# One layer of a hybrid encoder on one core: scaling of attention probabilities and masked decay tiles moved to VectorE, a second inverse tile, another order of DeltaNet pieces

## The chip, the cores and the metric

The kernel runs on one core of one Trainium2 chip. The time is device time in microseconds (us) of one launch. TensorE (PE in the profile) multiplies, VectorE (DVE), ScalarE (ACT) and GpSimd (POOL) do everything elementwise, SyncE (SP) issues all DMA transfers of this kernel in one queue. PEld is TensorE's loading of weights, which runs beside its matmuls.

## The reference

One layer with 1024 tokens of width 1024 in float32: a mixer (windowed attention and a bidirectional gated DeltaNet side by side, from one input projection), cross attention into 256 memory tokens, and a SwiGLU network, each with normalisation and residual. The change lies in the mixer:

```python
h = _rms_norm(x, g_mix_pre); proj = h @ w_in            # 1024 x 1024 @ 1024 x IN_COLS
# windowed attention, 8 heads, 2 key/value heads, blocks of 128, +-1 block:
scores = jnp.where(mask, einsum(q, k) * 64 ** -0.5, -inf)
m = max(max(scores), sink); p = exp(scores - m)
o = einsum(p / (sum(p) + exp(sink - m)), v)
...
# DeltaNet, 4 heads of 128, both directions, chunks:
q, k, v = silu(conv5(proj[...])), q and k L2-normalised
g = cumsum(-exp(a_log) * softplus(a + dt_bias)); beta = sigmoid(bt)
decay = exp(where(lower_triangle, g[i] - g[j], -inf))
lower = strict_lower((k * beta) @ k.T * decay); tmat = lower + I
u, w = tmat^-1 @ [v * beta, k * beta * exp(g)]
qk = q @ k.T * decay
scan over chunks: v_new = u - w @ S; o = q exp(g) @ S + qk @ v_new; S = S * g_last + kg.T @ v_new
...
mix = concat([attn_o, dn_o]) @ w_out; x += norm(mix); then cross attention, then SwiGLU
```

## The kernel before

Every large product is written as three fp32r matmuls of a high and a low part (`hhi,whi`, `hlo,whi`, `hhi,wlo`); `whi` is cast on ScalarE (L103) and `wlo` subtracted on VectorE or GpSimd (L104). The input projection is cut into pieces of 128 output columns (`proj`, matmuls at L260, 1056 of 128x128 by 128x512 after the first stage), and between these pieces stands the work that uses them.

The program is written as lists of pieces, and a tile scheduler reorders the instructions of each engine from that text, the tiles' pools and its own idea of durations. ORDER_1 holds the DeltaNet preparation; a letter with a head's number is one piece: q, k and v are projection plus convolution (`delta_proj`: copies and scaled sums, L282 to L286), E the decays, K the turned keys, U the key products (to `d_u` in memory), S the beta rows of two heads, C the query products (to `d_pz` and `d_kv`), B the inverse of the 32 x 32 diagonal blocks of two heads. ORDER_2 holds the attention projections A, V, the gate G, the levels L (which put together the full inverse of a head from B's blocks, in memory `d_inv`) and windows W, two windows at a time. ORDER_3 holds the scans with the remaining windows between them. Then come the output projection (L1029), cross attention and the SwiGLU network, which the change doesn't touch.

`decays(h)` makes, for both halves b of the chunks and both directions, a mask tile times one column per chunk, for the high and the low part of g: tile `gm` (128 x 4 x 128), eight tiles for a head. TensorE multiplies each with a triangular matrix (L471), four into one bank, and ScalarE takes the exponential (E, L474).

`base_inverse(g)` loads the diagonal blocks of two heads into V, makes A from them, runs 30 steps of small VectorE products (L539, L541), writes V and A once more (L543, L544) and stores both. V and A come from the pool `tb` with one buffer, so the second inverse takes the space of the first. `levels(h)` fetches the blocks again (`cz`, `cw`), makes m5, c5, c6 of them, and passes through `bs`, `z5`, `mov6` between PE and ACT or DVE (L589 to L616).

`window(n, g)` loads queries (`qr`), splits them (`qs`, the low part by GpSimd at L641), scores them (`psw`), takes the maximum on VectorE (L651), exponentials on ScalarE (L658), the reciprocal of the sum (`es`, L661 to L664), scales the four probability tiles of 128 x 384 or 128 x 256, and in a second part transposes them (`ptw`), splits them (`ph` on ScalarE L103, `pl` on VectorE L104) and multiplies with the values (`pow`, L677).

Of the kernel before, what the change touches and what calls it, by code (L numbers as in the profile page):

```python
# [10 lines left out]
F32 = mybir.dt.float32  # L11
# [3 lines left out]
ALU = mybir.AluOpType  # L15
# [4 lines left out]
P = 128  # L20
# [3 lines left out]
NT = S // P  # L24
# [9 lines left out]

ORDER_1 = ("k0 k1 q0 E0 K0 U0 E1 v0 K1 U1 S0 q1 C0 v1 E2 C1 k2 E3 k3 q2 K2 U2 v2 K3 U3 S1 q3 C2 v3 C3 B0 B1").split()
ORDER_2 = "L0 L1 G0 G1 A4 V A0 A1 L2 L3 W W W A2 A3 G2 G3 W".split()
ORDER_3 = ("M " + "s01 W K " * 5 + "s01 K " * 3 + "s01 V V").split()

# [36 lines left out]
def tile_hybrid_block(  # L77
# [6 lines left out]
    nc = tc.nc  # L84
# [9 lines left out]
    def f32(ap):  # L94
        return ap.bitcast(F32)

    def bc(ap, axis, shape):
        return ap.unsqueeze(axis).to_broadcast(list(shape))
# [10 lines left out]
    def pool(name, bufs, **kw):  # L109
        return tc.tile_pool(name=name, bufs=bufs, reuse_waits="tile", **kw)  # L110
# [28 lines left out]
    C0, C1 = _AT["mUi"], _AT["mU"]  # L139
# [14 lines left out]
    cm = {n: (C[:, a - C0:a - C0 + P] if a < C1 else CE[:, a - C1:a - C1 + P]) for n, a in _AT.items() if n != "ident"}  # L154
# [115 lines left out]
    pp_ = ExitStack()  # L270
    tb = pp_.enter_context(pool("tb", 1))
# [125 lines left out]

    pa1.close()
    pa0.close()

# [58 lines left out]
    def decays(h):  # L461

        for b in range(2):
            pa = small()
            n = 0
            for d, (mi, ml) in enumerate((("mUi", mL_r), ("mLi", mU_r))):
                for part in (ghi, glo):
                    gm = t2.tile([P, 4, P], F32R, tag="gm", name="gm")
                    for j in range(4):
                        nc.scalar.activation(gm[:, j, :], cm[mi], AF.Identity, scale=part[:, d, h, 4 * b + j:4 * b + j + 1])  # L470
                    nc.tensor.matmul(pa, ml, gm.rearrange("p c n -> p (c n)"), start=(n == 0), stop=(n == 3))  # L471
                    n += 1
            E = Es[h, b] = t2.tile([P, 4, P], F32, tag="E", name="E", bufs=4)
            nc.scalar.activation(E, pa.rearrange("p (c n) -> p c n", c=4), AF.Exp)  # L474
# [40 lines left out]
    def base_inverse(g):  # L515

        V = tb.tile([P, 32, 32], F32, tag="V", name="V", bufs=1)
        for q in range(4):  # L520
            r = slice(32 * q, 32 * q + 32)
            nc.sync.dma_start(V[q:64:4], d_u[g].rearrange("h c p n -> (h c) p n")[:, r, r])
        bB = tb.tile([P, 32], F32, tag="bB", name="bB", bufs=1)
        b1 = tb.tile([64, 32], F32, tag="b1", name="b1", bufs=1)
        bv = d_beta[g].rearrange("(d h c) (b s) -> d (h c b) s", d=2, h=2, b=4)
        for d in range(2):
            nc.sync.dma_start(bB[64 * d:64 * d + 64], bv[d])
        nc.sync.dma_start(b1, bv[1])
        A = tb.tile([P, 32, 32], F32, tag="A", name="A", bufs=1)
        nc.vector.scalar_tensor_tensor(A[0:64], V[0:64].rearrange("p r s -> p s r"), -1.0,  # L530
                                       bc(bB[0:64], 1, (64, 32, 32)), ALU.mult, ALU.mult)
        nc.vector.scalar_tensor_tensor(A[64:128], V[0:64], -1.0, bc(b1, 1, (64, 32, 32)), ALU.mult, ALU.mult)
        nc.gpsimd.affine_select(out=A, in_=A, compare_op=ALU.is_gt, fill=0.0, base=0,
                                pattern=[[1, 32], [-1, 32]], channel_multiplier=0)
        tmp = tb.tile([P, 256], F32, tag="tmpb", name="tmpb", bufs=1)
        for j in range(1, 31):
            n = 31 - j
            tv = tmp[:, 0:n * j].rearrange("p (r s) -> p r s", r=n)
            nc.vector.tensor_tensor(tv, A[:, j + 1:, j:j + 1].to_broadcast([P, n, j]),  # L539
                                    A[:, j:j + 1, 0:j].to_broadcast([P, n, j]), ALU.mult)  # L540
            nc.vector.tensor_tensor(A[:, j + 1:, 0:j], A[:, j + 1:, 0:j], tv, ALU.add)  # L541
        nc.gpsimd.memset(A.rearrange("p r s -> p (r s)")[:, 0:1024:33], 1.0)
        nc.vector.tensor_tensor(V.rearrange("p r s -> p s r"), A, bc(bB, 2, (P, 32, 32)), ALU.mult)  # L543
        nc.gpsimd.tensor_tensor(A, A, bc(bB, 2, (P, 32, 32)), ALU.mult)  # L544

        for i in range(2):
            for d in range(2):
                nc.sync.dma_start(d_inv[g][i][d].rearrange("h c b r s -> (h c b) r s"),
                                  (A if i == d else V)[64 * d:64 * d + 64])
# [77 lines left out]
    def window(n, g):  # L627

        tok = slice(n * P, (n + 1) * P)
        k0, k1 = max(n - 1, 0), min(n + 1, NT - 1) + 1  # L630
        nb = k1 - k0
        w = nb * P
        band = C[:, _AT["band0"] - C0 + (k0 - n + 1) * P:][:, 0:w]

        khi, klo = (t[:, k0 * P:k1 * P] for t in keys[g])
        qr = tw.tile([P, 4, P], F32, tag="qr", name="qr", bufs=1)
        for r in range(2):
            nc.sync.dma_start(qr[64 * r:64 * r + 64], d_q[256 * g:256 * g + 256, tok].rearrange("(h e) t -> e h t", h=4))
        qs = tw.tile([P, 4, P], F32R, tag="qs", name="qs")
        nc.scalar.copy(qs, qr)  # L640
        nc.gpsimd.tensor_tensor(qs[64:128], qr[64:128], f32(qs[64:128]), ALU.subtract)  # L641

        m4 = tw.tile([P, 4], F32, tag="m4", name="m4")
        ssum = tw.tile([P, 4], F32, tag="ssum", name="ssum")
        pr = []
        for hh in range(4):
            pp = pw.tile([P, 512], F32, tag="pw", name="psw")
            for i, kk in enumerate((khi, klo)):
                nc.tensor.matmul(pp[:, 0:w], qs[:, hh, :], kk, start=(i == 0), stop=(i == 1))
            sc = tw.tile([P, 384], F32, tag="sc", name="sc", bufs=8)  # L650
            nc.vector.tensor_tensor_reduce(out=sc[:, 0:w], in0=pp[:, 0:w], in1=band, scale=0.125,  # L651
                                           scalar=sink[:, 4 * g + hh:4 * g + hh + 1], op0=ALU.add, op1=ALU.max,
                                           accum_out=m4[:, hh:hh + 1])
            pr.append(sc)
        nm = tw.tile([P, 4], F32, tag="nm", name="nm")
        nc.vector.tensor_scalar(nm, m4, -1.0, None, ALU.mult)
        for hh in range(4):
            nc.scalar.activation(pr[hh][:, 0:w], pr[hh][:, 0:w], AF.Exp, bias=nm[:, hh:hh + 1],  # L658
                                 accum_out=ssum[:, hh:hh + 1])
        es = tw.tile([P, 4], F32, tag="es", name="es")  # L660
        nc.gpsimd.tensor_tensor(es, sink[:, 4 * g:4 * g + 4], m4, ALU.subtract)  # L661
        nc.scalar.activation(es, es, AF.Exp)
        nc.vector.tensor_tensor(es, es, ssum, ALU.add)
        nc.vector.reciprocal(es, es)  # L664
        for hh in range(4):
            nc.scalar.mul(pr[hh][:, 0:w], pr[hh][:, 0:w], es[:, hh:hh + 1])
        yield
        po = pw.tile([P, 4, P], F32, tag="pow", name="pow", bufs=1)
        for j in range(nb):
            pp = pw.tile([P, 512], F32, tag="pw", name="ptw")  # L670
            for hh in range(4):
                nc.tensor.transpose(pp[:, hh * P:(hh + 1) * P], pr[hh][:, j * P:(j + 1) * P], ident)
            ph = tw.tile([P, 512], F32R, tag="ph", name="ph")
            pl = tw.tile([P, 512], F32R, tag="pl", name="pl")
            split(ph, pl, pp)
            for i, pe_ in enumerate((ph, pl)):
                nc.tensor.matmul(po.rearrange("p h t -> p (h t)"), vhl[:, k0 + j, g].rearrange("p r e -> p (r e)"), pe_,  # L677
                                 start=(j == 0 and i == 0), stop=(j == nb - 1 and i == 1))
        ao = tw.tile([P, 4, P], F32, tag="ao", name="ao", bufs=1)[0:64]
        nc.scalar.copy(ao, po[64:128])  # L680
        nc.vector.tensor_tensor(ao, po[0:64], ao, ALU.add)
        nc.sync.dma_start(d_mix[g * 256:(g + 1) * 256, tok].rearrange("(h e) t -> e h t", e=64), ao)
# [38 lines left out]
    def issue(order, table):  # L721
        for o in order:
            table[o[0]](*(int(c) for c in o[1:]))

    issue(ORDER_1, {**{n: delta_proj(n) for n in "kqv"}, "E": decays, "K": turned_keys, "U": key_products, "S": beta_rows,
                    "C": query_products, "B": base_inverse})
# [337 lines left out]
    for hf in range(2):  # L1064
        for kp in range(4):
            k2 = slice(2 * kp, 2 * kp + 2)
# [73 lines left out]
    q0 = cross_q(0)  # L1140
    cross_attention(q0)
    q1 = cross_q(1)
# [68 lines left out]
    for e in range(EARLY):  # L1211
        f = 2 * e
        sg = te.tile([P, 512], F32, tag="sg", name="sg0")
        w, A = [], []
# [318 lines left out]
```

## Time and profile before

| | us |
|---|---|
| median of three runs | 1563.44 (1560.02 to 1566.67) |
| the profiled execution, own time | 1564.91 |
| its span (first to last instruction) | 1562.9 |
| TensorE busy | 1496.5 |
| VectorE busy | 1041.0 |
| ScalarE busy | 789.0 |
| GpSimd busy | 369.3 |
| mean granted TensorE clock | 0.988 of full speed |

A row of the timeline gives the start in us, the duration, engine, line, operation, out<-in, shapes and a count where equal instructions follow each other; in brackets stands how long the engine had been idle and what released it. Rows of waits give the total, the number and the longest. In the program of before, the lines are those of the function listing above; from the first edit on, those of the changed program are higher by 1 (from L400), 4 (from L474) and 5 to 7 (from L666).

### The profile page before, as it was taken

The page shows a single profiled execution, that of the slowest core. Times are in us where ns is not written, and L with a number is a line of the kernel's source. Part 1 is how long each engine was busy: PE and PEld are TensorE (multiplying, and loading weights), DVE is VectorE, ACT ScalarE, POOL GpSimd, SP SyncE. Part 2 cuts the span into 40 slices and gives each one's busy share as a digit, 9 for nine tenths or more (in the row PEclk, how much of TensorE's full clock was granted, in tenths as well). Part 3 has the DMA queues.
Part 4 walks back from the last instruction along what each step waited for, and adds up shares of the span by engine and source line. Part 5 has one row for each costly group of instructions (what it writes and reads, how often), then busy time and mean ns, then how long its engine had stood idle before and what let it go on. Part 6 is the DMA issues. An engine that isn't in the chain of part 4 may idle for free.

```text
span 1562.9 us, 21101 instructions
## 1 busy us (share of the span) xinstructions
PE 1496.5 (96%) x7451; PEld 1255.6 (80%) x7451; DVE 1041.0 (67%) x1664; ACT 789.0 (50%) x1634; POOL 369.3 (24%) x364
## 2 busy tenths in 40 slices
PE   6999999898899989999999999999999999999997
PEld 5877878787899877788888777888888888888786
DVE  6747989775788865444355458786867654696665
ACT  5698933357757774554345575332322322454542
POOL 3001220011236300153202221433534333000021
PEclk9999999999899999999999999999999999999999
DMA  6224575763998484454213164343434333853354
GB/s 203 75 82 124 154 202 132 175 187 122 316 279 283 136 279 175 135 198 153 68 55 126 50 222 149 121 135 121 135 115 141 101 102 133 292 194 102 108 173 163
DMA packets 264710, 242.95 MB, mean 155 GB/s; under 512 B 33800, under 2 KB 203677, under 8 KB 264605
## 3 DMA queue, kind: packets, MB, share of 16 engines
q1 hardware_dynamic: 264605, 241.62, 49.1%
q8 instruction: 58, 0.95, 0.3%
q14 instruction: 47, 0.39, 0.1%
HBM read 172.07 MB, written 66.88 MB: 153 GB/s over the span
## 4 chain that ended last, share of the span: by engine, by line
PE 66%; DVE 7%; ACT 6%; DMA 6%; issue 2%; SPq 2%; POOL 1%; DVEq 0%; POOLq 0%; ACTq 0%
PE pmg L1029 9%; PE pD L1204 8%; PE pE L1204 7%; PE pA L1204 6%; PE pcq L260 6%; PE pdX L1394 6%; PE pdA L1394 4%; PE pB L1204 4%; PE psc L798 3%; PE pdD L1394 2%; PE pg L260 2%; PE pcs L1110 1%; PE pco L1136 1%; PE pdX L1487 1%; PE pck L929 1%
## 5 line engine op out<-in xcount | busy, mean ns | idle before, releaser
L103 ACT CAST whi<-wraw 128x1024 fp32r<-128x1024 f32 x108 | 113.1, 1048 | 142.8 <-PE pmg L1029 33.7
L104 DVE TENSOR_TENSOR wlo<-wraw,whi 128x1024 fp32r<-128x1024 f32 x70 | 85.7, 1225 | 95.2 <-ACT whi L103 91.1
L260 PE MATMUL pg<-hhi,whi 128*128 128x512 f32 x352 | 140.4, 399 | 0.0
L260 PE MATMUL pg<-hhi,wlo 128*128 128x512 f32 x352 | 139.4, 396 | 0.0
L260 PE MATMUL pg<-hlo,whi 128*128 128x512 f32 x352 | 139.4, 396 | 0.0
L104 POOL TENSOR_TENSOR wlo<-wraw,whi 128x1024 fp32r<-128x1024 f32 x38 | 92.5, 2434 | 167.7 <-ACT whi L103 157.9
L1029 PE MATMUL pmg<-whi,b 128*128 128x512 f32 x384 | 118.5, 395 | 2.6 <-ACT whi L103 2.2
L1204 PE MATMUL pA<-s,whi 128*128 128x512 f32 x352 | 109.5, 392 | 1.3 <-ACT m L1221 1.3
L1029 PEld LDWEIGHTS pmg<-whi,b 128*128 128x128 f32 x384 | 71.2, 188 | 17.9 <-ACT whi L103 2.7
L260 PEld LDWEIGHTS pg<-hhi,wlo 128*128 128x128 f32 x352 | 67.0, 190 | 13.3
L260 PEld LDWEIGHTS pg<-hlo,whi 128*128 128x128 f32 x352 | 66.9, 190 | 13.2
L1394 PE MATMUL pdX<-dhl,whi 128*128 128x512 f32 x264 | 76.1, 390 | 1.5 <-ACT dhl L103 0.8
L1204 PEld LDWEIGHTS pA<-s,whi 128*128 128x128 f32 x352 | 65.3, 188 | 15.0 <-ACT m L1221 2.0
L260 PEld LDWEIGHTS pg<-hhi,whi 128*128 128x128 f32 x352 | 66.9, 190 | 13.1 <-ACT hhi L103 0.2
L103 ACT CAST whi<-araw 128x1024 fp32r<-128x1024 f32 (+1 forms) x36 | 35.4, 982 | 71.8 <-PE pdX L1394 27.6
L1029 PE MATMUL pmg<-wlo,b 128*128 128x512 f32 x192 | 71.5, 392 | 0.0
L1281 POOL TENSOR_TENSOR act<-act,up 128x512 f32<-128x512 f32 x33 | 50.2, 1520 | 88.8 <-DVE up L1280 53.5
L1204 PE MATMUL pA<-s,wlo 128*128 128x512 f32 x176 | 68.7, 391 | 1.0 <-DVE wlo L104 1.0
L104 DVE TENSOR_TENSOR wlo<-araw,whi 128x1024 fp32r<-128x1024 f32 (+1 forms) x36 | 40.8, 1134 | 39.4 <-ACT whi L103 39.3
L285 DVE SCALAR_TENSOR_TENSOR acc<-cp,cols,acc 128x1024 f32<-128x1024 f32 x48 | 63.9, 1332 | 1.4 <-ACT acc L283 0.8
L1253 POOL TENSOR_TENSOR sr<-wraw 128x512 f32<-128x512 f32 x22 | 30.4, 1381 | 127.1 <-DMA wraw<-in_w_gate_up_dram 127.1
L1394 PEld LDWEIGHTS pdX<-dhl,whi 128*128 128x128 f32 x264 | 49.3, 188 | 12.7 <-ACT dhl L103 1.1
(411 smaller groups left out, 4096.7 us busy)
## 6 DMA issues: line engine op xcount, KB each, us to landing
wraw<-in_w_gate_up_dram SPq DMA_DIRECT2D x52, 512.0 KB, 3.9
kv<-d_kv SPq DMA_DIRECT2D x32, 512.0 KB, 6.3
wraw<-in_w_in_dram SPq DMA_DIRECT2D x22, 512.0 KB, 4.1
b<-in_w_down_dram SPq DMA_DIRECT2D x20, 512.0 KB, 6.5
araw<-d_as SPq DMA_DIRECT2D x20, 512.0 KB, 3.7
pz<-d_pz SPq DMA_DIRECT2D x32, 256.0 KB, 6.7
wraw<-in_w_ckv_dram SPq DMA_DIRECT2D x16, 512.0 KB, 7.6
wraw<-in_w_out_dram SPq DMA_DIRECT2D x16, 512.0 KB, 4.1
```

Of the source, the lines that this page charges most:

```text
L103: nc.scalar.copy(hi, src)
L104: (eng or nc.vector).tensor_tensor(lo, src, f32(hi), ALU.subtract)
L260: nc.tensor.matmul(p_, w[:, k, :], ah[a][:, k, :], start=(k == 0 and i == 0), stop=(k == nk - 1 and i == 2))
L285: nc.vector.scalar_tensor_tensor(acc, cp[:, t:t + S], taps[t], acc, ALU.mult, ALU.add)
L798: nc.tensor.matmul(out[:, d, h, :], lt[:, d, h, :], rt[:, d, h, :], start=True, stop=True)
L929: nc.tensor.matmul(pp, w[:, k, :], mT[a][:, k, :], start=(k == 0 and i == 0), stop=(k == KT - 1 and i == 2))
L1029: nc.tensor.matmul(pp[t], act[a][:, k, tt], w_[:, kk, :], start=(k == 0 and i == 0), stop=(k == KT - 1 and i == 2))
L1110: nc.tensor.matmul(pp[:, t2_, :], q[a][:, ct, tt], kr_[b_][:, ct, :], start=(j == 0 and i == 0), stop=(j == 1 and i == 2))
L1204: nc.tensor.matmul(out_, w[a][:, k, :], xx[b_][:, k, :], start=(start and k == 0 and i == 0), stop=(k == HK - 1 and i == 2), skip_group_ch ...
L1253: nc.gpsimd.tensor_tensor(s[0], b_[:, 0:HK], b_[:, HK:], ALU.add)
L1281: nc.gpsimd.tensor_tensor(o_, o_, up, ALU.mult)
L1394: nc.tensor.matmul(banks[t], a[:, k - k0, tt], w, start=(first and k == 0 and i == 0), stop=(k == NB - 1 and i == 2), skip_group_check=not ...
```

## The change

Four edits. In ORDER_1 the query and value pieces of the first head, q0 and v0, move from the start to behind S0. In `decays`, the eight gm tiles of each of the first two heads are made by one VectorE product each, of two broadcast operands, instead of four ScalarE instructions. In `base_inverse`, the second inverse's V gets a pool of its own, `tb1`. In `window`, the first eight windows (all of the first key/value head) scale their four probability tiles on VectorE instead of ScalarE.

```diff
-ORDER_1 = ("k0 k1 q0 E0 K0 U0 E1 v0 K1 U1 S0 q1 C0 v1 E2 C1 k2 E3 k3 q2 K2 U2 v2 K3 U3 S1 q3 C2 v3 C3 B0 B1").split()
+ORDER_1 = ("k0 k1 E0 K0 U0 E1 K1 U1 S0 q0 v0 q1 C0 v1 E2 C1 k2 E3 k3 q2 K2 U2 v2 K3 U3 S1 q3 C2 v3 C3 B0 B1").split()
...
+    tb1 = pp_.enter_context(pool("tb1", 1))
...
-                    for j in range(4):
+                    if h < 2:
+                        nc.vector.tensor_tensor(gm, bc(part[:, d, h, 4 * b:4 * b + 4], 2, (P, 4, P)), bc(cm[mi], 1, (P, 4, P)),
+                                                ALU.mult)
+                    for j in range(4 if h > 1 else 0):
                         nc.scalar.activation(gm[:, j, :], cm[mi], AF.Identity, scale=part[:, d, h, 4 * b + j:4 * b + j + 1])
...
-        V = tb.tile([P, 32, 32], F32, tag="V", name="V", bufs=1)
+        V = (tb1 if g else tb).tile([P, 32, 32], F32, tag="V", name="V", bufs=1)
...
-            nc.scalar.mul(pr[hh][:, 0:w], pr[hh][:, 0:w], es[:, hh:hh + 1])
+            if g * NT + n < 8:
+                nc.vector.tensor_scalar(pr[hh][:, 0:w], pr[hh][:, 0:w], es[:, hh:hh + 1], None, ALU.mult)
+            else:
+                nc.scalar.mul(pr[hh][:, 0:w], pr[hh][:, 0:w], es[:, hh:hh + 1])
```

How the built programs differ is seen in the engines' orders. VectorE, behind the gates' arithmetic at about 70 us, where the first convolutions stand. A name's number tells tiles of one name apart. Before:

```order
L349 COPY beta_557<-za_541 128x8x8
L104 TENSOR_TENSOR wlo_1004<-wraw_1001,whi_1003 128x1024
L285 SCALAR_TENSOR_TENSOR acc_696<-cp_693,cols_71,acc_696 128x1024
L409 TENSOR_SCALAR nEG_627<-EG_576 128x64
L285 SCALAR_TENSOR_TENSOR acc_696<-cp_693,cols_71,acc_696 128x1024 x3
L104 TENSOR_TENSOR wlo_1146<-wraw_1143,whi_1145 128x1024
L285 SCALAR_TENSOR_TENSOR acc_928<-cp_925,cols_71,acc_928 128x1024 x2
L492 TENSOR_TENSOR U_799<-ps_800,E_732 128x512
```

After:

```order
L471 TENSOR_TENSOR gm_641<-ghi_563,C_75 128x512
L349 COPY beta_557<-za_541 128x8x8
L471 TENSOR_TENSOR gm_644<-glo_564,C_75 128x512
L104 TENSOR_TENSOR wlo_959<-wraw_956,whi_958 128x1024
L285 SCALAR_TENSOR_TENSOR acc_876<-cp_873,cols_71,acc_876 128x1024 x2
L471 TENSOR_TENSOR gm_647<-ghi_563,C_75 128x512
L471 TENSOR_TENSOR gm_650<-glo_564,C_75 128x512
L285 SCALAR_TENSOR_TENSOR acc_876<-cp_873,cols_71,acc_876 128x1024
L410 TENSOR_SCALAR nEG_630<-EG_576 128x64
L285 SCALAR_TENSOR_TENSOR acc_876<-cp_873,cols_71,acc_876 128x1024
L471 TENSOR_TENSOR gm_656<-ghi_563,C_75 128x512
L471 TENSOR_TENSOR gm_659<-glo_564,C_75 128x512
```

The masked products stand between the first key head's convolution and the second's; the last of the 16 stands six rows ahead of the second head's last U.

SP's queue around the loads of the second inverse's V. Before:

```order
L504 DMA d_pz11_104<-pm_1881 128x4x128
L548 DMA d_inv00_107<-V_2071 64x1024
L548 DMA d_inv01_108<-V_2071 64x1024
L126 DMA wraw_2729<-in_w_in_dram 128x8x128
L548 DMA d_inv00_107<-A_2081 64x1024
L548 DMA d_inv01_108<-A_2081 64x1024
L522 DMA V_2153<-d_u1_106 16x32x32 x4
L527 DMA bB_2158<-d_beta1_112 64x32 x2
```

After:

```order
L497 DMA d_u1_106<-U_1726 128x4x128
L526 DMA V_2108<-d_u1_106 16x32x32 x4
L436 DMA d_beta1_112<-bT_1740 32x128
L552 DMA d_inv00_107<-V_2026 64x1024
L552 DMA d_inv01_108<-V_2026 64x1024
L532 DMA b1_2114<-d_beta1_112 64x32
L552 DMA d_inv00_107<-A_2036 64x1024
L552 DMA d_inv01_108<-A_2036 64x1024
```

The four loads now stand ahead of the first inverse's stores, right behind the last U that they read.

ScalarE at the levels: the rows from the casts of keys to `z5` of the second level (`bs` and `z5` belong to it, `m5` and `c6` to the third). Before:

```order
L103 CAST khi_3236<-kraw_3233 128x1024
L600 COPY bs_2454<-ps_2449 128x4x32
L600 COPY bs_2461<-ps_2456 128x4x32
L569 COPY m5_2963<-cz0_2959 32x256 x2
L572 COPY c6_2965<-cw0_2961 64x256
L569 COPY m5_2963<-cz1_2960 32x256 x2
L572 COPY c6_2965<-cw1_2962 64x256
L609 ACTIVATE z5_2468<-ps_2463 128x128
```

After:

```order
L103 CAST khi_3192<-kraw_3189 128x1024
L103 CAST vhl_2205<-ptv_2752 128x8x64
L576 COPY c6_2921<-cw1_2918 64x256
L576 COPY c6_2921<-cw0_2917 64x256
L604 COPY bs_2410<-ps_2405 128x4x32
L604 COPY bs_2417<-ps_2412 128x4x32
L573 COPY m5_2919<-cz1_2916 32x256
L573 COPY m5_2919<-cz0_2915 32x256
L573 COPY m5_2919<-cz1_2916 32x256
L573 COPY m5_2919<-cz0_2915 32x256
L613 ACTIVATE z5_2424<-ps_2419 128x128
```

The third level's c6 now stands ahead of the second level's bs. In TensorE's order the levels move up among the projections: the matmul of the second level that waits for `mov6` had 878 of the 1056 projection matmuls ahead of it, and has 835 and 852 (for its two halves). The first product with a gm tile has 157 ahead in both, the second head's first gm 241 before and 233 after, the third head's 351 and 322. Of ScalarE's 29 loads of function tables 27 are left.

## The prediction

> **What bounds the kernel now.** I read the page first, for who is busy:
>
> ```profile
> span 1562.9 us, 21101 instructions
> ...
> PE 1496.5 (96%) x7451; PEld 1255.6 (80%) x7451; DVE 1041.0 (67%) x1664; ACT 789.0 (50%) x1634; POOL 369.3 (24%) x364
> ```
>
> TensorE (PE) bounds the kernel. All that another engine can give back lies in 1562.9 - 1496.5 = 66.4 us of idle PE, plus what a low clock costs while PE is busy. The change touches only the pieces up to the end of the windows at 567 us, so next come the waits of PE before 600 us, summed (total, times, longest):
>
> ```profile
> PE pow L677 <- ACT ph L103: 11.4, 8, 3.6
> PE ps L471 <- ACT gm L470: 4.8, 4, 2.5
> PE ps L598 <- DVE mov L616: 4.7, 3, 3.3
> PE ps L589 <- DMA Ul<-d_u: 3.0, 1, 3.0
> PE pow L677 <- DVE pl L104: 2.8, 5, 1.5
> ...
> PE ps L441 <- ACT E L474: 0.2, 1, 0.2
> ```
>
> These are the pieces of the diff: decays wait for masked tiles (L471), levels for the inverse's data (L589, L598), windows for the split probabilities (L677). The first five together are 26.7 us, 1.7% of the time: a ceiling, not a forecast. The third view is busy time by stretch (columns PE, PEld, DVE, ACT, POOL, PEclk, DMA share, GB/s), to see which engine has room for work that is handed over:
>
> ```profile
> 50.00:100.00 50.00, 49.91 (x241) 41.16 (x240) 29.68 (x44) 41.63 (x101) 4.00 (x12) 1.00 0.29 82
> 100.00:150.00 50.00, 47.20 (x243) 38.78 (x243) 30.60 (x33) 40.59 (x114) 6.87 (x13) 1.00 0.38 107
> 150.00:200.00 50.00, 47.52 (x254) 40.28 (x253) 47.10 (x88) 47.73 (x142) 12.87 (x18) 1.00 0.51 148
> ...
> 350.00:400.00 50.00, 42.05 (x232) 35.40 (x231) 30.91 (x74) 38.59 (x87) 6.42 (x10) 0.91 0.55 166
> 400.00:450.00 50.00, 46.64 (x353) 45.03 (x352) 35.93 (x96) 31.54 (x72) 13.94 (x10) 0.92 0.91 292
> ```
>
> From 50 to 150 VectorE (DVE) is 60% busy and ScalarE (ACT) 82%; from 150 to 200 both are nearly full, so nothing can be handed over there. In the windows DVE has 14 to 19 us of room in each 50.
>
> **The masked tiles.** Of the four waits of L471, the timeline of PE has the last two as
>
> ```profile
> 115.35 0.50 PE L471 MATMUL ps<-gm,mL_r 128*128 128x512 f32 x1 [1.47 <-ACT gm L470]
> ...
> 153.78 0.50 PE L471 MATMUL ps<-gm,mU_r 128*128 128x512 f32 x1 [2.48 <-ACT gm L470]
> ```
>
> The first three (the group's 4.8 less 2.48: 2.32 us) belong to the second head, whose tiles move to DVE; the fourth to the third head, whose tiles stay on ACT. Prices, from the groups by line and form (ns min/median/max):
>
> ```profile
> L470 ACT ACTIVATE gm<-C,ghi x64: 384/395/466, 69.6 to 177.4; 128x128 fp32r<-128x128 f32 x64
> ...
> L503 DVE TENSOR_TENSOR pm<-pc,C x16: 680/683/693, 133.0 to 223.1; 128x512 f32<-128x512 f32 x16
> ...
> L666 ACT ACTIVATE sc<-sc,es x64: 492/606/652, 329.3 to 566.7; 128x384 f32<-128x384 f32 x48, 128x256 f32<-128x256 f32 x16
> ...
> L385 DVE TENSOR_SCALAR ang<-ang,CE x2: 483/484/486, 39.6 to 47.4; 128x512 f32<-128x512 f32 x2
> ```
>
> ACT loses 64 of these instructions, 64 x 395 ns = 25 us if each stood alone; in a run of four they overlap (the row at 152.47 below: four in 1.27 us), so 16 x 1.2 = about 19 us. DVE gains 16 products of one mask with a broadcast column. No such product is in the trace; L503 is the nearest (same size, two SBUF inputs, one of them broadcast): 16 x 0.683 = 10.9 us. Bounds: L385's 484 ns would make 7.7, one L104 of half size (1225/2 ns) 9.8; with the repeat along the inner axis it could be twice L503, 21.9. I take 10.9. It goes into 72 to 117 us, where the order has all 16 tiles. What DVE waits for from 70 to 130:
>
> ```profile
> DVE wlo L104 <- ACT whi L103: 18.5, 4, 7.6
> DVE U L492 <- ACT E L474: 9.7, 2, 6.1
> ```
>
> That is 28.2 us of DVE idling behind the very queue that gets shorter, so 10.9 fit and 21.9 still would. Wait by wait: 2.32 us go. For the fourth, ACT and DVE show why it was late:
>
> ```profile
> 149.51 1.06 ACT L286 ACTIVATE acc<-acc 128x1024 f32<-128x1024 f32 x1 [4.59 <-DVE acc L285]
> ...
> 152.47 1.27 ACT L470 ACTIVATE gm<-C,ghi 128x128 fp32r<-128x128 f32 x4
> ```
> ```profile
> 146.00 3.47 DVE L285 SCALAR_TENSOR_TENSOR acc<-cp,cols,acc 128x1024 f32<-128x1024 f32 x2
> ```
>
> ACT stood 4.59 us behind a convolution sum on DVE, with a cast, two copies and the third head's tiles queued behind. The new order puts k1 and its chain ahead of q0 and v0, so the third head's matmuls have 322 projection matmuls ahead of them on PE instead of 351. Whether DVE is clear of convolutions then can't be read; I take 1.5 of 2.48 as gone, bounds 0 and 2.48. With the 0.2 us of L441, which waits for E behind the same queue, 2.32 + 1.5 + 0.2 = 4.0 us are gained, bounds 2.3 and 5.0. The steps that pass q0 and v0 take with them GpSimd's sums of squares and, on SP's queue, the stores of kt, U and the beta rows, which now stand ahead of later weights and hold these up until ACT and DVE deliver. No wait of PE for a weight's DMA is among the rows above and the DMA share is 0.29 to 0.38 there: 0, with 1 us as the bound for one late weight. PE's work is unchanged.
>
> **The second inverse's tile and the levels.** PE, DVE, ACT and PE again, from the timeline:
>
> ```profile
> 235.69 1.37 PE L589 MATMUL ps<-ident,Ul 128*128 128x128 f32 x8 [2.98 <-DMA Ul<-d_u]
> ...
> 237.80 0.63 PE L260 MATMUL pg<-hlo,whi 128*128 128x512 f32 x1
> 238.23 0.63 PE L260 MATMUL pg<-hhi,wlo 128*128 128x512 f32 x1
> ...
> 241.69 0.39 PE L260 MATMUL pg<-hhi,whi 128*128 128x512 f32 x1
> 241.92 0.40 PE L260 MATMUL pg<-hlo,whi 128*128 128x512 f32 x1
> ```
> ```profile
> 128.60 0.69 DVE L492 TENSOR_TENSOR U<-ps,E 128x512 f32<-128x512 f32 x1 [3.66 <-ACT E L474]
> ...
> 219.90 1.22 DVE L532 SCALAR_TENSOR_TENSOR A<-V,b 64x1024 f32<-64x1024 f32 x1 [0.99 <-DMA V<-d_u]
> ...
> 277.44 2.09 DVE L543 TENSOR_TENSOR V<-A,bB 128x1024 f32<-128x1024 f32 x1
> ```
> ```profile
> 290.57 0.82 ACT L569 COPY m<-cz 32x256 f32<-32x256 f32 x2 [7.18 <-DMA cz<-d_inv]
> ```
> ```profile
> 299.59 0.66 PE L598 MATMUL ps<-mov,L 128*128 128x64 f32 x2 [3.28 <-DVE mov L616]
> ```
>
> DVE waited 0.99 us for V, loaded behind the first inverse's stores; with a tile of its own the load goes ahead of them. That alone moves no matmul: the second inverse ends at 279.5, 57 us after L532, in a chain of small DVE steps that the order shortens by starting earlier. U's last product (128.6 before, by the row order near 116 now) is followed by about as much DVE work up to the inverse's end in both orders, so I estimate that end near 264 instead of 279.5. The consumers move up too: the matmul with the 3.28 us wait had 878 projection matmuls ahead and has 835 to 852, 26 to 43 less at 0.23 us (241.69 to 241.92): 6 to 10 us. The chain, 15 us earlier, would then be early enough. But on ACT the second level's bs now stands behind copies that wait for the third level's fetch, the kind of wait that cost ACT 7.18 us at 290.57. Between the two I cost the levels at 0, with both ends from the waits there: -6 (2.98 and 3.28 go; the bit of slow PE after 235.69, some eight matmuls at 0.43 instead of 0.23, makes it 1.6 more where all goes) to +5 (they stay, and bs adds ACT's 7.18 less some 2 us of other matmuls that PE still has ahead of it, an estimate).
>
> **The windows.** PE's largest wait there, and ACT's queue ahead of it:
>
> ```profile
> 376.95 1.28 ACT L658 ACT_TABLE_LOAD   x1
> ...
> 380.77 1.28 ACT L771 ACT_TABLE_LOAD   x1
> ```
> ```profile
> 383.19 0.50 PE L677 MATMUL pow<-ph,vhl 128*128 128x512 f32 x1 [3.58 <-ACT ph L103]
> ```
> ```profile
> 380.00:390.00 10.00, 5.99 (x18) 4.47 (x19) 4.68 (x13) 9.79 (x20) 1.83 (x4) 0.70 0.68 226
> ```
>
> Eight windows move 4 scalings each. ACT loses about 2.1 us per window (four L666 at 606 ns, overlapped), 17 us, and two table loads that the new order no longer has (2.6). DVE gains 32 scalings of 384 or 256 elements: L385's 484 ns for 512 scaled by length gives 363 for 384, unscaled 484; I take 418, 32 x 0.418 = 13.4 us, bounds 11.6 and 15.5, in a stretch with 14 or more idle. But in the chain ahead of 383.19 no L666 stands: table load, exponentials, table load, gate, split. So less ACT work shortens that wait only by the table load. The scaled tiles come 0.4 us x 4 on DVE instead of 0.53 x 4 on ACT, and ACT can take the next split meanwhile; of the 11.4 + 2.8 us of L677 about 13 fall in windows of the first group by the timeline. I take 3 us, the two table loads and a little; bounds: 9 gained (two thirds of 13, with the clock's part of 380 to 390) and 4 lost (DVE's pl, the 2.8 us row, waits behind scalings once more per window).
>
> GpSimd can hold VectorE up. POOL and DVE:
>
> ```profile
> 376.58 1.28 POOL L641 TENSOR_TENSOR qs<-qr,qs 64x512 fp32r<-64x512 f32 x1 [18.49 <-DVE m L651]
> ```
> ```profile
> 376.95 0.95 DVE L656 TENSOR_SCALAR nm<-m 128x4 f32<-128x4 f32 x1
> ```
>
> A DVE scaling of four columns took 0.95 us and ended within 0.04 us of the GpSimd operation. A new scaling that meets a qs subtraction can so be held for up to 1.28 us, 8 x 1.28 = 10.2 us if each window has one such meeting; DVE's idle time covers that, unless the held scaling is the one PE waits for.
>
> **Sum.** 4.0 + 0 + 3 = 7.0 us; the later windows, whose code is unchanged, 0 with +-3 for another order. The profiled execution took 1564.9, 2.0 over its span and 1.5 over the median of 1563.4: 1564.9 - 7.0 - 1.5 = 1556.4.
>
> **Rivals.** First, the windows give up most of their waits: 4 + 9 = 13, and 1 of the levels': 1549. For it: ACT is busy 9.79 of 10 us from 380 to 390, and PE's clock is .70 there. Against: L666 isn't in the chain of 383.19.
>
> Second, what the decays gain is given back at the levels: PE arrives there 4 us earlier and the data don't, so the waits of 2.98 and 3.28 grow by those 4, and the windows keep half of their 3: 1563.4 - 1.5 = 1562. For it: both engines are 95% busy from 150 to 200. Against: DVE's 28.2 idle us ahead of that.
>
> Third, GpSimd's hold falls on the path: one meeting in each of eight windows, each on the tile that PE waits for next, turns the 7.0 gained into 3.2 lost: 1566.6. For it: the two rows above. Against: GpSimd is busy 6.4 and 13.9 us of 50 there. The Trainium skill, page "SBUF — State Buffer", section "Who interferes with whom", states this as a rule: a VectorE tensor_scalar in a two-port mode and a GpSimd operation exclude each other for the whole instruction, whichever came first holding the ports. The trace agrees, with 0.95 us for four columns. By the rule the new scalings are all exposed to it and the time may become this rival's, 1566.6; by the idle time of VectorE in the windows it stays the forecast's.
>
> Fourth, slower: the masked products make VectorE's chain to the inverses the bound. If they cost 21.9 us and the 28.2 idle us don't shrink (casts come no earlier, for ACT serves convolutions first), the inverse's end, 12 us earlier by the order, is 10 later; its consumers, 6 to 10 earlier, wait about 18 longer, less the 7: 1563.4 + 11 = 1574. It outweighs the gain from 21.9 - 11 = 11 us of products that nothing absorbs; at L503's price, 10.9, the two are equal. L503's row speaks against the double price, the idle rows against the rest.
>
> **Chances.** Forecast (1551 to 1560) 0.42, given back 0.20, windows 0.20, GpSimd 0.08, slower 0.10. The measurement can tell 0.5%, 7.8 us: faster is below 1555.6, slower above 1571.3. The forecast's case lies on that line and counts a little over half as faster, 0.23: faster 0.23 + 0.20 = 0.43; same 0.19 + 0.20 + 0.08 = 0.47; slower 0.10. The range, 1546 to 1568, takes in the windows' case, the given-back one and GpSimd's with some spread, and leaves out the slower one and the outer part of the windows' case.
>
> **What would show it.** The profile after should have no L471 wait near 100 to 117, gm products on DVE at 0.68 us, and U's products earlier. The second inverse's L547 should end near 264. ACT should be down 36 to 39 us in all, DVE up 24. The L677 waits should keep their place and lose about 3 us. I am wrong if gm takes over 1 us on DVE, if the L598 waits pass 7 us, or if the L677 waits fall below 6.

## The result and the profile after

The changed kernel takes 1553.81 us (median of five, 1550.21 to 1554.17) where the kernel before, run beside it, takes 1561.16 (five, 1559.40 to 1566.67). The ratio is 0.9938, 95% interval 0.9923 to 0.9953: faster by 0.5 to 0.8%. The forecast's ratio was 1556.4 / 1563.4 = 0.9955.

The profiled execution of after took 1550.21, its span is 1548.5. It stands 3.6 us under its median, that of before 3.8 over the median of five; so the spans differ by 14.4 us, about twice what the medians differ by, and a few us in one stretch of one trace decide nothing. The page after (busy time), then the waits of PE before 600 us:

```profile
PE 1491.4 (96%) x7451; PEld 1251.4 (81%) x7451; DVE 1057.6 (68%) x1712; ACT 753.9 (49%) x1536; POOL 364.7 (24%) x364
```
```profile
PE pow L684 <- ACT ph L103: 7.3, 4, 4.0
PE ptw L679 <- DVE m L655: 3.0, 6, 1.1
PE psw L653 <- DVE m L655: 3.0, 4, 1.3
...
PE ps L602 <- DVE mov L620: 1.6, 3, 0.8
PE psw L653 <- POOL qs L645: 1.5, 1, 1.5
PE ps L602 <- DVE L L595: 1.3, 1, 1.3
PE ps L593 <- DVE Z L625: 0.8, 1, 0.8
PE ps L475 <- ACT gm L474: 0.7, 1, 0.7
```

Of the waits that the prediction named, the masked tiles' went from 4.8 to 0.7, the levels' 2.98 for Ul is gone (the 0.8 at its line is for another tile, Z), their 4.7 for mov6 went to 1.6, the windows' wait for ph from 11.4 to 7.3, and that for pl is no longer on the list. In the windows others came: for the maxima m (L655), 1.7 and 0.8 before, 3.0 and 3.0 now. Busy time by stretch, after (columns as before):

```profile
100.00:150.00 50.00, 49.86 (x265) 42.25 (x264) 39.63 (x61) 42.58 (x122) 6.26 (x15) 1.00 0.51 143
150.00:200.00 50.00, 49.25 (x257) 41.68 (x256) 47.10 (x75) 38.11 (x106) 10.91 (x19) 1.00 0.60 162
200.00:250.00 50.00, 49.03 (x256) 40.90 (x255) 46.99 (x99) 18.80 (x51) 2.38 (x3) 1.00 0.59 153
250.00:300.00 50.00, 47.92 (x246) 40.16 (x245) 38.94 (x76) 13.91 (x31) 2.08 (x2) 0.93 0.68 171
300.00:350.00 50.00, 45.87 (x251) 38.40 (x250) 37.99 (x86) 22.95 (x55) 7.66 (x8) 1.00 0.55 158
350.00:400.00 50.00, 41.10 (x247) 35.48 (x246) 27.55 (x73) 31.06 (x74) 7.32 (x9) 0.90 0.75 221
400.00:450.00 50.00, 49.02 (x397) 47.04 (x396) 45.48 (x127) 23.94 (x56) 14.81 (x10) 1.00 0.95 307
```

and the same of before where it wasn't shown:

```profile
200.00:250.00 50.00, 46.94 (x230) 39.15 (x228) 44.30 (x80) 16.84 (x42) 6.79 (x5) 0.97 0.79 201
250.00:300.00 50.00, 46.05 (x250) 39.01 (x249) 41.89 (x93) 14.95 (x37) 2.07 (x2) 0.99 0.59 150
300.00:350.00 50.00, 48.24 (x262) 41.70 (x262) 36.95 (x78) 25.66 (x63) 6.36 (x6) 0.94 0.64 174
```

PE's idle time, the window less the first number behind the comma: from 100 to 200 it fell from 5.3 to 0.9 us, from 200 to 300 from 7.0 to 3.1, from 300 to 450 it stayed (13.1 and 14.0). The granted clock there rose: the shares missing before, 0.06, 0.09 and 0.08 of 50 us each, make 11.5 us, the 0.10 of 50 after 5.0; from 200 to 300 it is 2.0 before and 3.5 after. So 8.3 us of the spans' difference come from idle time between 100 and 300 us, 1.5 go back to the clock from 200 to 300, and 5.6 come from 300 to 450, the windows: 6.5 by the clock less 0.9 of idle time. Cross attention's first `pcq` matmul (L260), in code that the change doesn't touch, starts at 659.6 instead of 673.8: the 14 us are there by then. VectorE's masked products and the last full-size steps of the two inverses, after:

```profile
L471 DVE TENSOR_TENSOR gm<-ghi,C x8: 679/686/694, 69.7 to 106.3; 128x512 fp32r<-128x512 f32 x8
```
```profile
L547 DVE TENSOR_TENSOR V<-A,bB x2: 1985/2026/2067, 184.0 to 257.5; 128x1024 f32<-128x1024 f32 x2
```

The products take 686 ns and the second inverse's step starts at 257.5 instead of 277.4. All these are readings of one execution of each program; what repeats in a second one stands below, with the runs on the order.

### The profile page after: what moved, and what is told of

Read it like the earlier page. It is cut to its first block, busy times and chain, and to the rows that moved or that the text cites. A ratio compares the mean times of both kernels' runs of the same rounds, so it can differ in the third digit from the quotient of the medians.

```text
span 1548.5 us, 21052 instructions
## 1 busy us (share of the span) xinstructions
PE 1491.4 (96%) x7451; PEld 1251.4 (81%) x7451; DVE 1057.6 (68%) x1712; ACT 753.9 (49%) x1536; POOL 364.7 (24%) x364
## 5 line engine op out<-in xcount | busy, mean ns | idle before, releaser
L260 PE MATMUL pg<-hhi,whi 128*128 128x512 f32 x352 | 140.3, 399 | 0.0
L260 PE MATMUL pg<-hlo,whi 128*128 128x512 f32 x352 | 139.6, 397 | 0.0
L260 PE MATMUL pg<-hhi,wlo 128*128 128x512 f32 x352 | 138.6, 394 | 0.0
L104 POOL TENSOR_TENSOR wlo<-wraw,whi 128x1024 fp32r<-128x1024 f32 x38 | 92.3, 2430 | 175.3 <-ACT whi L103 175.2
L260 PEld LDWEIGHTS pg<-hhi,whi 128*128 128x128 f32 x352 | 66.7, 190 | 13.2 <-ACT hhi L103 0.2
L260 PEld LDWEIGHTS pg<-hhi,wlo 128*128 128x128 f32 x352 | 66.6, 189 | 13.3
L260 PEld LDWEIGHTS pg<-hlo,whi 128*128 128x128 f32 x352 | 66.6, 189 | 12.7
L285 DVE SCALAR_TENSOR_TENSOR acc<-cp,cols,acc 128x1024 f32<-128x1024 f32 x48 | 62.0, 1294 | 0.1
```

The costliest lines, as they stand in the source:

```text
L104: (eng or nc.vector).tensor_tensor(lo, src, f32(hi), ALU.subtract)
L260: nc.tensor.matmul(p_, w[:, k, :], ah[a][:, k, :], start=(k == 0 and i == 0), stop=(k == nk - 1 and i == 2))
L285: nc.vector.scalar_tensor_tensor(acc, cp[:, t:t + S], taps[t], acc, ALU.mult, ALU.add)
```

## The experiments

All ratios are to the kernel before, run beside, with 95% intervals. The first four do one edit alone.

**Scaling alone.**

```diff
-            nc.scalar.mul(pr[hh][:, 0:w], pr[hh][:, 0:w], es[:, hh:hh + 1])
+            if g * NT + n < 8: nc.vector.tensor_scalar(pr[hh][:, 0:w], pr[hh][:, 0:w], es[:, hh:hh + 1], None, ALU.mult)
+            else: nc.scalar.mul(...)
```

> Only the fourth edit on the kernel before: the first eight windows' probabilities scaled on VectorE. The sum of the prediction gives it 3 us (ratio about 0.998). If the windows carry the whole result, it gives 7 us or more (0.9955 or less) and the L677 waits of PE fall from 14.2 to below 10 us. If the result comes from the pieces ahead of the windows, it gives 0 with +-2 (0.9987 to 1.0013).

1.0009 (0.9995 to 1.0024). Nothing; the 3 us of the prediction's sum (0.998) lie outside the interval. The waits of `pow` did fall below 10, as the second case of the expectation asked: for ph to 6.5 us from 300 to 560 (11.4 before), for pl off the list. The time didn't follow, for others took their place: the scores' for m, pl and qs (5.4 us) and the scans' for vn (2.0).

**Masked tiles alone.**

```diff
+                    if h < 2: nc.vector.tensor_tensor(gm, bc(part[...], 2, (P, 4, P)), bc(cm[mi], 1, (P, 4, P)), ALU.mult)
-                    for j in range(4):
+                    for j in range(4 if h > 1 else 0):
```

> Only the masked tiles of the first two heads on VectorE, in the old order of pieces. The prediction's sum gives the 2.3 us of the second head's waits (ratio 0.9985), with or without part of the third head's 2.48. If VectorE's chain to the inverses suffers for want of the new order, the levels' waits grow from 7 us by up to 10.9 us and the kernel is slower by 3 to 8 us (1.002 to 1.005).

0.9942 (0.9922 to 0.9961): as much as the whole change, and more than either theory gave it. The largest waits of PE from 40 to 300 us, and VectorE's last step of the inverses:

```profile
PE psw L652 <- POOL qs L644: 1.4, 1, 1.4
PE ps L601 <- DVE L L594: 1.2, 2, 0.8
PE ps L441 <- ACT acc L286: 1.2, 1, 1.2
PE ps L474 <- ACT gm L473: 0.9, 2, 0.7
```
```profile
L546 DVE TENSOR_TENSOR V<-A,bB x2: 1985/2020/2054, 183.3 to 258.5; 128x1024 f32<-128x1024 f32 x2
```

The masked tiles' wait fell from 4.8 to 0.9, Ul's 2.98 and mov6's 3.28 are gone, and the inverse ends about as early as in the whole change, in the old order of pieces and with the shared tile. The third head's first matmul with a masked tile has 322 projection matmuls ahead of it here too, instead of 351.

**Order alone.**

```diff
-ORDER_1 = ("k0 k1 q0 E0 K0 U0 E1 v0 K1 U1 S0 q1 ...
+ORDER_1 = ("k0 k1 E0 K0 U0 E1 K1 U1 S0 q0 v0 q1 ...
```

> Only the new order of the DeltaNet pieces. The prediction's sum gives it part of the third head's wait, 0 to 2.5 us (0.9984 to 1.0). A rival, that the order is what brings the inverses' data earlier: the levels' waits of 2.98 and 3.28 us and the slow clock behind them go, 5 to 7 us (0.9955 to 0.997). A third, that without the masked tiles on VectorE the order only pushes the second head's tiles into ScalarE's full queue: 2 to 5 us slower.

0.9998 (0.9984 to 1.0013). In the built program TensorE's rows are those of before but for the name of one tile:

```order
-L432 MATMUL ps<-ident,bp_992 32x128
+L432 MATMUL ps<-ident,bp_853 32x128
```

The scheduler had already drawn k1's chain ahead of q0 and v0. In the traces the instructions of all engines and the DMA issues are those of before, in the same order, by their operations and tiles: the text's order moves nothing, and this run is a second execution of the program of before. The masked tiles' waits are the same:

```profile
PE ps L471 <- ACT gm L470: 4.8, 4, 2.5
PE ps L589 <- DMA Ul<-d_u: 2.3, 1, 2.3
PE ps L598 <- DVE mov L616: 2.1, 3, 0.8
```

With TensorE's rows the same, mov6's waits up to 300 us are 2.1 us here and 3.3 before (the row of 299.59), Ul's 2.3 and 2.98: by about that much one execution differs from another. By stretch:

```profile
300.00:350.00 50.00, 46.47 (x252) 40.11 (x251) 36.79 (x77) 24.59 (x61) 6.24 (x6) 0.93 0.65 178
350.00:400.00 50.00, 42.71 (x233) 36.11 (x233) 31.02 (x74) 39.66 (x89) 6.33 (x10) 0.87 0.55 160
400.00:450.00 50.00, 47.16 (x368) 45.17 (x368) 37.34 (x104) 30.39 (x69) 14.74 (x10) 0.96 0.96 306
```

Idle time and missing clock together, what TensorE loses, are 25.7 us in the windows here and 24.6 before; from 200 to 300 they are 6.9 and 9.0.

**Own tile alone.**

```diff
-        V = tb.tile([P, 32, 32], F32, tag="V", name="V", bufs=1)
+        V = (tb1 if g else tb).tile([P, 32, 32], F32, tag="V", name="V", bufs=1)
```

> Only the own tile for the second inverse. The prediction's sum gives it 0, for VectorE waited 0.99 us for that load and the matmuls that use the result come 57 us later: 1.0 +-0.001. If the load's place on the queue sets the levels' waits, 3 to 6 us faster (0.996 to 0.998).

1.0004 (0.9992 to 1.0015), though its inverse's last step starts at 272.4 instead of 277.4. The trace shows one way in which such a gain is lost: the last `pow` matmul starts at 565.0 instead of 575.6, but the output projection at 575.3 instead of 577.6, for a wait that neither execution of before has:

```profile
575.27 1.22 PE L1030 MATMUL pmg<-whi,s 128*128 128x512 f32 x2 [4.44 <-ACT vv L950]
```

The next four take one edit out of the whole change (the diffs are those above, reversed).

**All but the scaling.**

> The changed kernel without the scaling on VectorE (order, masked tiles and own tile stay). The prediction's sum: 4 us faster than before (ratio 0.9974), 3 us less than the whole change. If the windows carry the result: 1.0 to 0.999. If the pieces ahead of them carry it: 0.994 to 0.995, the same as the whole.

0.9950 (0.9932 to 0.9968). Within the interval of the whole change. Against the two measurements of the changed program, 0.9938 and 0.9918 (below), it is 1.9 and 5.0 us slower with intervals that overlap, so that the scaling gives something inside the change is neither shown nor ruled out. PE's wait for ph from 300 to 560 us is 2.1 us here, with the scaling on ScalarE, and 7.3 in the change:

```profile
PE pck L933 <- ACT whi L103: 2.5, 2, 1.6
PE pcv L949 <- ACT whi L103: 2.2, 1, 2.2
PE pow L681 <- ACT ph L103: 2.1, 2, 1.9
```

But the waits don't add up to less: others (for casts of cross attention's weights) stand ahead of it, and TensorE idles 12.9 us from 300 to 450 (14.0 in the change). A shorter wait for ph isn't a shorter kernel.

**All but the masked tiles.**

> The changed kernel with all masked tiles on ScalarE again. The prediction's sum: 3 to 4.5 us faster than before (0.997 to 0.998). If the order needs VectorE's masked tiles (ScalarE's queue holds the second head's tiles and E on the path), the L471 waits rise from 4.8 us to 7 or more and the gain goes: 0.999 to 1.002.

0.9957 (0.9941 to 0.9973): order, own tile and scaling together gain 0.3 to 0.6%, and each alone nothing. So the masked tiles are enough for the gain, but not needed for a part of it. The masked tiles' wait is back (4.9 us), the inverse's last step starts at 272.0, and the 4.44 us lost by the own tile alone don't occur (the output projection starts at 569.9). Which of the scheduler's choices makes the difference isn't shown.

**All but the order.**

> The changed kernel with the old order of pieces. The prediction's sum: 5 to 6 us faster than before (0.996 to 0.9968). If the order is what brings the inverse's data earlier, the levels' waits of 2.98 and 3.28 us come back and grow with VectorE's 10.9 us: 0.999 to 1.003.

0.9918 (0.9900 to 0.9936), overlapping the whole change's interval. The inverse's last step starts at 257.7. Here too the traces' instructions and DMA issues are, engine by engine, those of the changed kernel in the same order, so this is the changed program measured a second time:

```profile
300.00:350.00 50.00, 47.08 (x250) 39.66 (x249) 36.69 (x85) 21.88 (x53) 8.64 (x8) 0.97 0.56 158
350.00:400.00 50.00, 40.43 (x245) 34.79 (x244) 27.54 (x73) 31.69 (x76) 7.40 (x10) 0.90 0.75 221
400.00:450.00 50.00, 49.02 (x396) 47.04 (x395) 45.38 (x127) 24.02 (x56) 14.81 (x10) 1.00 0.94 308
```

That gives three things. The first of the four edits does nothing, in the old kernel and in the changed one. Two measurements of one program differ by 0.2%, so the other three runs of this group, from 0.9930 to 0.9957, lie too close to be ranked. And what TensorE loses from 300 to 450 us repeats, 24.6 and 25.7 us in the two executions of before, 19.0 and 20.0 in the two of after, while from 200 to 300 it is 9.0 and 6.9 against 6.5 and 6.3.

**All but the own tile.**

> The changed kernel with the two inverses sharing V's space again. The prediction's sum: the same as the whole change, 0.994. If the second inverse's earlier end depends on the tile: the end moves back from 259.5 us by 5 us or more and the ratio is 0.996 to 0.998.

0.9930 (0.9912 to 0.9949), the whole change's time, though the inverse's last step starts 3.9 us later (261.4). Like the tile alone: it moves the inverse by 4 or 5 us, and nothing of it is seen in the time.

The last four go further than the change.

**The masked products twice.**

```diff
-                    if h < 2:
+                    for _ in range(2 if h < 2 else 0):
                         nc.vector.tensor_tensor(gm, ...)
```

> The changed kernel with each of the 16 masked products on VectorE issued twice, the second over the first with the same values: 11.0 us more of VectorE between 70 and 110 us, with TensorE's order the same but for a few rows. If VectorE's idle time absorbs it, as the prediction held for up to 21.9 us: the ratio of the whole change, 0.994 +-0.0015, no L471-kind wait of PE over 1 us, and the second inverse ends within 3 us of 259.5. If VectorE's chain is the bound (the fourth rival), the inverse ends some 11 us later, the levels wait, and the ratio is 0.999 to 1.003.

0.9986 (0.9971 to 1.0002): most of the gain is gone, some 7 us. There is no wait of PE for masked tiles over 1 us, but the inverse's last step starts 31 us later than in the change, 11 later than before:

```profile
L547 DVE TENSOR_TENSOR V<-A,bB x2: 2028/2066/2105, 213.4 to 288.5; 128x1024 f32<-128x1024 f32 x2
```
```profile
L475 PE MATMUL ps<-gm,mL_r x16: 389/390/504, 72.3 to 175.3; 128*128 128x512 f32 x16
```

The expectation is wrong on one point: TensorE's order isn't the same. The scheduler counted the longer products and set the third and fourth heads' masked matmuls to about where before has them (the last of this form, the fourth head's, at 175.3; 161.5 in the change, 174.6 before). That isn't where the time goes: TensorE idles 0.8 us from 100 to 200 and 2.4 from 200 to 300, as little as in the change (0.9 and 3.1). The loss stands in the windows:

```profile
300.00:350.00 50.00, 44.76 (x226) 36.74 (x225) 38.79 (x89) 25.04 (x58) 5.92 (x6) 0.93 0.71 187
350.00:400.00 50.00, 42.46 (x245) 36.63 (x244) 37.11 (x95) 32.30 (x77) 6.65 (x10) 0.86 0.72 219
400.00:450.00 50.00, 44.79 (x342) 43.02 (x339) 38.54 (x110) 25.00 (x55) 15.52 (x11) 0.93 0.89 270
```

18.0 us idle and 14.0 by the clock, 32.0 together, against 19.0 and 20.0 for the changed program. The last projection matmul starts at 359 instead of 367, so fewer of them are left for the windows; that this is the reason isn't shown, and the run doesn't separate VectorE's 11 us from the scheduler's answer to them.

**All four heads' masked tiles on VectorE.**

```diff
-                    if h < 2:
+                    if h < 4:
...
-                    for j in range(4 if h > 1 else 0):
+                    for j in range(4 if h > 3 else 0):
```

> The changed kernel with the masked tiles of all four heads on VectorE: 11 us more there, most of it between 120 and 180 us, where VectorE was 94% busy. If VectorE has no room there, as the prediction said, the inverses end 5 to 11 us later and the ratio rises to 0.996 to 1.001. If what counts is the emptying of ScalarE's queue, it falls to 0.990 to 0.993.

0.9961 (0.9945 to 0.9978), the inverse's last step at 281.4, 24 us later than in the change and not 5 to 11. That fits what the prediction read from 150 to 200 us, where VectorE is 94% busy (from 120 to 180 it is 88% in the change). Emptying ScalarE's queue further gains nothing; that it costs isn't sure, for the interval touches the change's.

**All sixteen windows' scaling on VectorE.**

```diff
-            if g * NT + n < 8:
+            if g * NT + n < 16:
```

> The changed kernel with the scaling of all 16 windows on VectorE. The runs so far give the scaling of the first eight nothing by itself. If it is hidden work on either engine: 0.9925 to 0.9955. If VectorE, 92% busy from 400 to 500 us beside the scans, has no room for the other eight (13 us): 3 to 8 us slower than the change, 0.996 to 0.999.

0.9958 (0.9942 to 0.9974), between the two bands and overlapping the change's interval: inconclusive. If the other eight cost anything, it is at most some 8 us (0.9974 against the change's lower end of 0.9923).

**Queries' low part on VectorE.**

```diff
-        nc.gpsimd.tensor_tensor(qs[64:128], qr[64:128], f32(qs[64:128]), ALU.subtract)
+        nc.vector.tensor_tensor(qs[64:128], qr[64:128], f32(qs[64:128]), ALU.subtract)
```

> The changed kernel with the low part of the queries (L645) subtracted by VectorE instead of GpSimd, so that no scaling can meet that GpSimd instruction: 16 instructions of about 0.7 us more on VectorE. If the hold by GpSimd costs PE time (third rival), 2 to 10 us faster than the change: 0.988 to 0.9925. If the two meetings seen in the trace, some 2.7 us of VectorE, are covered by idle time: 0.993 to 0.996, for the VectorE work is about as long as the hold that goes.

0.9965 (0.9946 to 0.9983): not faster, a little above the second band, and overlapping the change's interval. If GpSimd's holds cost TensorE time, it is no more than the 16 subtractions cost on VectorE. None of the four is better than the change.

## Why the prediction came out right, and where its steps didn't

**The price of a masked product** was right: 686 ns against 683 from L503; eight gm rows above, eight more alike.

**The masked tiles' waits** were right in size: 4.0 forecast, 4.4 less idle time from 100 to 200 us (4.3 in the second executions). The prediction's 2.32 went, and the third head's 2.48 with it, where 1.5 were counted; a wait of 0.7 for a tile of the fourth head, at 161.50, is new.

**The cause of the third head's earlier place** was wrong, "The new order puts k1 and its chain ahead of q0 and v0". The order alone leaves the program as it was; the masked tiles alone bring the third head's matmuls to their earlier place and the inverse's last step to 258.5. What I read in the order of the changed program was the scheduler's answer to another edit. The estimate of the inverse's end, near 264, was near (257.5 + 2.1 = 259.6), for it was taken from the changed program's rows and not from the text. Its own rows give 267 rather than 264 (279.5 less 128.6 - 116), and the fourth rival counts with those 12 us; U's last product did come at 115.0, and the inverse by another 6 us earlier than that explains.

**The levels** were costed at 0 with ends of -6 and +5. In the first two traces they gained 3.9 us of idle time from 200 to 300 (2.4 after the clock's 1.5), in the second executions of the two programs 0.6; between those the size stays open, and 0 wasn't far off. Ul's wait for its data, 2.98 and 2.3 in the two executions of before, is gone in both executions of the changed program, but smaller waits for L, Z and mov6 stand in its place (2.9 us after). Of the two forces that I set against each other the earlier chain came out ahead; ScalarE's bs behind the third level's copies cost nothing in the one execution of the changed program and 1.1 us in the other.

**The windows** are the mis-sized term, and for the wrong cause: 3 us forecast for the scaling, none measured for it alone (1.0009), and none beyond the noise in the change (0.9938 and 0.9918 with, 0.9950 without, overlapping), while the stretch from 300 to 450 gained 5.6 us, 5.7 in the second executions, and as much where the scaling stays on ScalarE (all but the scaling: 17.9 us lost there, against 19.0 and 20.0). The prediction had the reason in hand: no L666 stands ahead of the longest wait. (Its "about 13" of the first group's waits are 10.7 in the same timeline, the eight waits of `pow` up to 425.70, so two thirds of them are 7, and the bound of 9 was too wide.) In the change it is the same again; ScalarE ahead of PE's longest wait there:

```profile
387.00 1.04 ACT L103 CAST whi<-wraw 128x1024 fp32r<-128x1024 f32 x1 [4.05 <-DMA wraw<-in_w_ckv_dram]
388.30 1.04 ACT L103 CAST khi<-kraw 128x1024 fp32r<-128x1024 f32 x1 [0.24 <-DMA kraw<-d_k]
389.25 0.61 ACT L662 ACTIVATE sc<-sc,nm 128x384 f32<-128x384 f32 x1
...
391.75 0.56 ACT L103 CAST ph<-ptw 128x512 fp32r<-128x512 f32 x1
```
```profile
392.36 0.79 PE L684 MATMUL pow<-ph,vhl 128*128 128x512 f32 x1 [4.00 <-ACT ph L103]
```

ScalarE was idle for 4.05 us behind a weight's transfer, with ph queued behind it, so in this place a ScalarE with less to do brings ph no earlier: it waits longer for what stands first in its queue. The waits for ph and pl fell by 6.9 us, those for m and qs rose by 5.0, and the windows' idle time stayed about as it was. The scaling's own price came out right by luck: 13.3 us in all by the eight groups, 13.4 forecast, but 2.6 of them are GpSimd's holds (below); without these it is 10.7, under the prediction's bound of 11.6.

**The signs** that the prediction named came in part. U's products are earlier, L547 ends at 259.6, and no wait for a masked tile is left at 100 to 117. ScalarE is down 35.1 us, a little under the 36 to 39. VectorE is up 16.6 where 24 were named: the new instructions last 24.3 us (11.0 and 13.3), but others got shorter, the convolution sums most (48 at L285, the longest 2.94 us before and 2.16 after). The waits at L677 lost 6.9 us instead of 3, and the time has that only in part.

**GpSimd's hold** occurs and hardly reaches PE. Two of the eight groups met a GpSimd instruction; VectorE, then GpSimd:

```profile
326.19 2.11 DVE L671 TENSOR_SCALAR sc<-sc,es 128x256 f32<-128x256 f32 x4
335.76 1.40 DVE L671 TENSOR_SCALAR sc<-sc,es 128x384 f32<-128x384 f32 x4
...
443.72 2.80 DVE L671 TENSOR_SCALAR sc<-sc,es 128x256 f32<-128x256 f32 x4
```
```profile
326.10 1.27 POOL L645 TENSOR_TENSOR qs<-qr,qs 64x512 fp32r<-64x512 f32 x1 [6.07 <-ACT qs L644]
```
```profile
443.21 2.37 POOL L104 TENSOR_TENSOR wlo<-wraw,whi 128x1024 fp32r<-128x1024 f32 x1 [4.18 <-ACT whi L103]
```

In the run with all sixteen windows the same first group met none:

```profile
325.80 1.14 DVE L671 TENSOR_SCALAR sc<-sc,es 128x256 f32<-128x256 f32 x4
```

The two held ones took 0.97 and 1.66 us more, 2.63 in all, where the rival had 10.2. The first GpSimd instruction ends at 327.37, the second at 445.58, and both groups end 0.93 us behind that. The Trainium skill, "SBUF — State Buffer", section "Who interferes with whom", states that of a VectorE instruction in a two-port mode and a GpSimd one, the first to issue holds the shared ports for its whole instruction and the other is blocked. The trace agrees: the first scaling of each of these groups ends 0.15 us behind the GpSimd instruction. That the scalings run in such a mode no row shows. The holds' price was a quarter of the rival's, and of it TensorE met 0.48 us: the maximum m that VectorE computes right behind the first held group comes late for a transpose. Behind the second group it waits for nothing up to 450.

```profile
328.90 1.19 PE L679 MATMUL ptw<-ident,sc 128*128 128x128 f32 x8 [0.48 <-DVE m L655]
```

**That VectorE's idle time would absorb up to twice the price** was wrong as a forecast of the time: 21.9 us of products give back most of the gain. The fourth rival comes out in part. With the double price the inverse does end 11 us later than before, where the rival had 10; but its consumers don't wait some 18 us longer (TensorE's waits for Ul and Z there are 3.6 us in all), the time isn't above that of before, and what is lost is lost in the windows. The 28.2 us of idle VectorE were a sum of gaps and not one store of room. Since the order moved too, how much is VectorE's own delay stays open.

So the direction and one term, the masked tiles' 4, were right for their reason, and the total, 7.0 us forecast and 7 to 12 measured (0.9953 to 0.9923 of 1561; the second measurement of the program gives 10 to 16), is near partly by luck: its 3 us for the windows stand for a cause that alone gives none, and meet a gain there that comes without it. That gain comes with the masked tiles alone too; that run's stretches:

```profile
300.00:350.00 50.00, 48.50 (x276) 42.23 (x275) 34.78 (x80) 29.65 (x70) 6.46 (x7) 0.97 0.58 152
350.00:400.00 50.00, 43.18 (x268) 37.13 (x267) 30.17 (x83) 44.80 (x98) 8.43 (x11) 0.93 0.77 231
400.00:450.00 50.00, 47.48 (x373) 45.75 (x372) 39.13 (x108) 30.80 (x71) 15.43 (x11) 0.97 0.98 314
```

10.8 us idle and 6.5 missing by the clock, 17.3 together, against 24.6 and 25.7 in the two executions of before and 19.0 and 20.0 in the two of after. It isn't the masked tiles' alone: the run with the own tile alone loses 18.4 there too, and gives it back later. Which of the windows' rows bring this isn't shown.

## What to carry to other kernels

Where a scheduler sets the order, don't credit a line of the text with a move that the built program shows: build each edit by itself, and compare the rows. Two programs with the same rows are one program, and their two times show what a difference is worth. Handing an instruction from a full engine to one with gaps paid here where TensorE waited for that instruction (the masked tiles), and by itself not where something else stood in the queue ahead of what the waiting matmul needs (the scaling); a wait that gets shorter can come back under another name. Edits that each measure nothing alone (own tile, scaling) gained 0.4% together, since each changes the scheduler's choices for the other; so runs of one edit alone and runs of all but one are both needed.

## What the runs showed of the hardware

A run of four VectorE scalings of 128x384 took 1.40 us, 0.35 each, less than the 0.41 that one record lasts by the median: the records overlap, and the starts lie 0.33 us apart. One scaling of 128x256 that met a GpSimd instruction lasted 2.01 us instead of 0.34 and ended 0.15 us behind that instruction's end at 445.58; in the run with sixteen windows the longest lasted 2.43. A product of two operands that are both broadcast, one along the inner axis, costs what one with a single broadcast costs (686 and 683 ns for 128x512).
